# Odd row pairs copied to both partition halves, one block apart, so that one 128-row matmul does two kinds of products (dilated convolution, fp32, one core)

## The chip, the cores and the metric

The kernel runs on 1 core of one Trainium2 chip. The metric is the device time of one execution in microseconds (us), as the median of the runs shown. Times in the text that have no other source are read from one profiled execution, in us from its first instruction. Engines: PE is TensorE (PEld its weight loads), DVE VectorE, ACT ScalarE, POOL GpSimd, SP SyncE. All transfers here are issued by SP and carried by 16 DMA engines.

## The reference

```python
batch, c_in, h, w, c_out, k, dilation = 16, 64, 64, 64, 128, 3, 2
# x (16, 64, 64, 64) fp32, weight (128, 64, 3, 3) fp32, pad = 2 on each side
for b, co, ci, kh, kw:
    output[b, co] += weight[co, ci, kh, kw] * x_pad[b, ci, kh*2:kh*2+64, kw*2:kw*2+64]
# output (16, 128, 64, 64) fp32
```

16.8 MB are read (x) and 33.6 MB written; the weights have 0.3 MB.

## The kernel before

**Layout.** Two images share the 128 partitions: image m = 0 has its 64 input channels on partitions 0 to 63, image m = 1 on 64 to 127. There are 8 such pairs of images (`pb`), each cut into 4 groups of 16 rows (`g`); `G` counts the 32 groups. A pair's x is loaded as fp32 (`x32`, three buffers), cast to fp16 by ACT in chunks (`cast`, `x16`), and the output of a pair (`o`, 128 output channels on the partitions, both images side by side) is stored as fp32.

**Fewer products.** Because the dilation is 2, rows are taken two at a time: a block is two rows, and blocks alternate between even (e = 0) and odd (e = 1). With W0, W1, W2 the three kernel rows, an even output block is W0 x[odd block before] + W1 x[even] + W2 x[odd], and an odd one W0 x[even] + W1 x[odd] + W2 x[even block after]. The kernel forms s = x[even] + x[odd] on DVE (`rowsum`, `xs`) and uses five products of three taps each instead of six:

- kind 0: P = W1 s, in the PSUM tile `psP`;
- kinds 1 and 2: psA = (W2 - W1) x[odd] + W0 x[odd block before];
- kinds 3 and 4: psB = (W0 - W1) x[even] + W2 x[even block after];
- even output rows = psA + P, odd output rows = psB + P.

**Matmuls.** `product` issues, for each of the three taps j, one matmul for either half of the partitions (`hb`): 64 rows of the array by 128 columns, 512 or 496 output columns. The two halves write different PSUM banks. A kind has 6 matmuls, a group 30. Kinds 2 and 4 leave out one block of four at the upper and the lower edge of an image (`z`).

**Per group,** in program order: PE does psP, psA, psB (in group 0 psP last); ACT copies psP to SBUF (`p_sb`, since psP has one buffer) and casts up to two chunks ahead (`casts`); DVE forms the next group's row sum and then the two sums psA + p_sb and psB + p_sb into `o`. psA, psB and the weights' PSUM tiles share three buffers.

**Weights.** At the start the weights are loaded (`w32`), combined to the five kinds (`wd`, on DVE, POOL and ACT), and `turn(k)` transposes kind k with narrow matmuls (64 columns) against an identity, into both halves of the partitions; a copy by ACT or DVE puts it into `w_sb`. `dummies` are matmuls on zeros beside it.

**Order.** The schedule is written by hand (`manual_schedule`): every engine executes its instructions in program order, and SP's transfers queue in program order too. SP's list is: weights, x of pairs 0, 1, 2; x of pair 3 in group 0; from then on each pair's stores when its groups are done and further loads between them (pair 4 after group 3, pair 5 in group 7, pair 6 in group 11, pair 7 in group 15). A load into an `x32` buffer waits until the casts of the pair that had it are done. The last pair is stored in two halves; of image 1's first half the last 8 rows (`ROWS4`) go as a transfer of 124 partitions and one of 4 (`FOUR`). By the trace's landings these two run on 4 of the 16 DMA engines each, the other stores on all 16.

Of the kernel before, what the change touches and what calls it, by code (L numbers as in the profile page):

```python
# [10 lines left out]
def kernel(  # L11
# [7 lines left out]
    nc = tc.nc  # L19

    B, CI, H, W = x.shape
    CO, CI_w, KH, KW = weight.shape
# [4 lines left out]
    d = 2  # L27

    P = 128
    f32 = mybir.dt.float32  # L30
    f16 = mybir.dt.float16
# [5 lines left out]
    NG = H // GR  # L37
    NBLK = GR // 4
    NH = GR // 2 * W
    npairs = B // 2  # L40
    ngroups = npairs * NG
# [3 lines left out]
    wpool = ctx.enter_context(tc.tile_pool(name="wpool", bufs=1))  # L45
# [6 lines left out]
    apool = ctx.enter_context(tc.tile_pool(name="apool", bufs=3, space=bass.MemoryType.PSUM))  # L52
# [6 lines left out]
    x32_tiles, x16_tiles, xs_tiles, o_tiles = {}, {}, {}, {}  # L59

    def load(pb, cuts=(0, H)):
        x32_tiles[pb] = fpool.tile([P, HW], f32, tag="x32", name="x32")
        for lo, hi in zip(cuts[:-1], cuts[1:]):
            nc.sync.dma_start(  # L64
                out=x32_tiles[pb][:, lo * W : hi * W], in_=x_pair[pb, :, lo * W : hi * W]
            )

    def cast(c):
        pb, g = divmod(c, NG)
        lo, hi = chunk_rows[g]  # L70
        if g == 0:
            x16_tiles[pb] = xpool.tile([P, HW], f16, tag="x16", name="x16")
        nc.scalar.copy(  # L73
            out=x16_tiles[pb][:, lo * W : hi * W], in_=x32_tiles[pb][:, lo * W : hi * W]
        )

    def rowsum(c):
        pb, g = divmod(c, NG)
        if g == 0:
            xs_tiles[pb] = sxpool.tile([P, HW // 2], f16, tag="xs", name="xs")  # L80
        v = x16_tiles[pb][:, g * GR * W : (g + 1) * GR * W].rearrange(
            "p (b e q) -> p b e q", e=2, q=2 * W
        )
        s = xs_tiles[pb][:, g * NH : (g + 1) * NH].rearrange("p (b q) -> p b q", q=2 * W)
        nc.vector.tensor_tensor(out=s, in0=v[:, :, 0], in1=v[:, :, 1], op=add)  # L85

    w32 = wpool.tile([CO, CI * KH * KW], f32, name="w32")
    nc.sync.dma_start(out=w32, in_=weight.rearrange("o i h w -> o (i h w)"))  # L88
    load(0, (0, 2 * GR + d, H))
# [1 line left out]
    load(2)  # L91
    zero = wpool.tile([P, 512], f16, name="zero")
    nc.vector.memset(zero, 0.0)  # L93
    ident = wpool.tile([P, P], f16, name="ident")
    make_identity(nc, ident)

# [2 lines left out]
    def dummies(n):  # L99
        for _ in range(n):  # L100
            nc.tensor.matmul(out=dm[:, 0:512], lhsT=zero[:, 0:P], rhs=zero)  # L101
# [6 lines left out]
    w_sb = wpool.tile([P, NT * CO], f16, name="w_sb")  # L108
# [7 lines left out]

    wts = [apool.tile([P, 1024], f32, tag="ab", name="wt") for _ in range(3)]

    def turn(k):
        c0 = k // 3 * 512  # L120
        for j in range(KW):
            t = k * KW + j
            for r in range(2):
                nc.tensor.matmul(  # L124
                    out=wts[k % 3][r * CI : (r + 1) * CI, c0 + j * CO : c0 + (j + 1) * CO],
                    lhsT=wd[:, t * CI : (t + 1) * CI],
                    rhs=ident,
                )
        return w_sb[:, k * KW * CO : (k + 1) * KW * CO], wts[k % 3][:, c0 : c0 + KW * CO]
# [2 lines left out]
    t0 = turn(0)  # L132
    dummies(2)
    nc.vector.tensor_copy(out=t0[0], in_=t0[1])
    t1 = turn(1)
    nc.scalar.copy(out=t1[0], in_=t1[1])  # L136
    t2 = turn(2)
    nc.vector.tensor_copy(out=t2[0], in_=t2[1])
    dummies(1)
    t3 = turn(3)  # L140
    t4 = turn(4)
    dummies(1)
    nc.vector.tensor_copy(  # L143
        out=x16_tiles[0][:, 8 * W : 18 * W], in_=x32_tiles[0][:, 8 * W : 18 * W]
    )
    nc.scalar.copy(out=x16_tiles[0][:, 0 : 8 * W], in_=x32_tiles[0][:, 0 : 8 * W])  # L146
    nc.scalar.copy(out=t3[0], in_=t3[1])
    nc.vector.tensor_copy(out=t4[0], in_=t4[1])
    rowsum(0)

    ahead = [1]
# [1 line left out]
    def casts(G):  # L153
        for n in range(2 if G else 3):
            c = ahead[0]
            if c >= ngroups or c > G + (7 if c < 2 * NG else 5):
                return
            cast(c)
            ahead[0] += 1

    def product(ps, src, kind, blk0, nblk, first, last):
        for j in (1, 0, 2):
            dw = (j - 1) * d
            o0, o1 = max(0, -dw), W - max(0, dw)
            t = kind * KW + j
            for hb in range(2):
                pp = slice(hb * CI, (hb + 1) * CI)
                rhs = src(pp, dw + o0, dw + o1)
                po = ps[:, hb * NH + blk0 * 2 * W : hb * NH + (blk0 + nblk) * 2 * W]
                po = po.rearrange("p (r w) -> p r w", w=W)[:, :, o0:o1]  # L170
                nc.tensor.matmul(  # L171
                    out=po,
                    lhsT=w_sb[pp, t * CO : (t + 1) * CO],
                    rhs=rhs,
                    start=first and j == 1,
                    stop=last and j == 2,
                )

    def blocks(x16, b0, n, e):
        v = x16.rearrange("p (b e r w) -> p b e r w", e=2, r=2, w=W)  # L180
        return lambda pp, c0, c1: v[pp, b0 : b0 + n, e, :, c0:c1]
# [8 lines left out]
    def store_both(pb, r0, r1):  # L190
        nc.sync.dma_start(
            out=out_img[2 * pb : 2 * pb + 2, :, r0 * W : r1 * W].rearrange("m o q -> o m q"),
            in_=o_tiles[pb].rearrange("p (m q) -> p m q", m=2)[:, :, r0 * W : r1 * W],
        )

    FOUR = ((0, P - 4), (P - 4, P))
    ROWS4 = 8

    for G in range(ngroups):
        pb, g = divmod(G, NG)  # L200
        x16 = x16_tiles[pb]
        xs = xs_tiles[pb].rearrange("p (r w) -> p r w", w=W)
        if g == 0:
            o_tiles[pb] = opool.tile([P, 2 * HW], f32, tag="osb", name="osb")
        o = o_tiles[pb].rearrange("p (m b e q) -> p m b e q", m=2, e=2, q=2 * W)
        b0 = g * NBLK

        def summed():
            ps = ppool.tile([P, 2 * NH], f32, tag="p", name="psP")
            sv = lambda pp, c0, c1: xs[pp, g * GR // 2 : (g + 1) * GR // 2, c0:c1]  # L210
            product(ps, sv, 0, 0, NBLK, True, True)
            return ps

        if G:
            psP = summed()

        psA = apool.tile([P, 2 * NH], f32, tag="ab", name="psA")
        product(psA, blocks(x16, b0, NBLK, 1), 1, 0, NBLK, True, False)
        z = 1 if g == 0 else 0
        product(psA, blocks(x16, b0 + z - 1, NBLK - z, 1), 2, z, NBLK - z, False, True)  # L220

        psB = apool.tile([P, 2 * NH], f32, tag="ab", name="psB")
        product(psB, blocks(x16, b0, NBLK, 0), 3, 0, NBLK, True, False)
        z = 1 if g == NG - 1 else 0
        product(psB, blocks(x16, b0 + 1, NBLK - z, 0), 4, 0, NBLK - z, False, True)

        if not G:
            psP = summed()

        if not G:  # L230
            casts(0)
        p_sb = spool.tile([P, 2 * NH], f32, tag="psb", name="p_sb")
        nc.scalar.copy(out=p_sb, in_=psP)  # L233
        if G:
            casts(G)
        if G + 1 < ngroups:
            rowsum(G + 1)
        pv = p_sb.rearrange("p (m b q) -> p m b q", m=2, q=2 * W)
        for e, ps in ((0, psA), (1, psB)):
            nc.vector.tensor_tensor(  # L240
                out=o[:, :, b0 : b0 + NBLK, e],
                in0=ps.rearrange("p (m b q) -> p m b q", m=2, q=2 * W),
                in1=pv,
                op=add,
            )

        if G == 0:
            load(XF)
        if g == NG - 1 and 0 < pb < npairs - XF - 1:
            load(pb + XF + 1, (0, H) if pb < 3 else (0, H // 2, H))  # L250
        if G == NG - 2:
            store(0, 1, 0, (NG - 1) * GR)
            store(0, 0, 0, (NG - 1) * GR)
        if G == NG - 1:
            store_both(0, (NG - 1) * GR, H)
            load(XF + 1)
        elif pb == npairs - 1:
            if g % 2 == 1:
                store(pb, 0, (g - 1) * GR, (g + 1) * GR)
                if g == 1:  # L260
                    store(pb, 1, 0, 2 * GR - ROWS4)
                    store(pb, 1, 2 * GR - ROWS4, 2 * GR, FOUR)
                else:
                    store(pb, 1, (g - 1) * GR, (g + 1) * GR)
        elif g == NG - 1:
            for m in (1, 0) if pb == 1 else (0, 1):
                store(pb, m)
# [37 lines left out]
```

## Time and profile before

| what | value |
|---|---|
| device time, median of 3 runs | 128.58 us (126.77, 128.58, 128.86) |
| profiled execution, first to last instruction (span) | 126.1 us; what lies around the span is not in the profile |
| PE busy / share of the span | 104.5 us / 83%, 1000 matmuls |
| DVE, ACT, POOL busy | 90.9, 64.9, 2.2 us |
| DMA moved | 50.78 MB, 403 GB/s mean over the span |
| mean granted PE clock | 0.949 (1.00 until about 112 us, then 0.5) |
| last matmul / last DVE instruction / last DMA packet end | 108.3 / 109.6 / 124.8 us |

A row of busy tenths divides the span into 40 equal slices; 9 means 90% or more. A line of groups has the instruction's line in the kernel, engine, operation, output <- input tiles, the count, busy time, the mean of one in ns, and the engine's idle time before them. The recorded length of a matmul includes the time that it spends in the array's pipeline, so that neighbouring matmuls overlap in the records; their starts tell the rate.

### The profile page before, as it was taken

Reading aid. Unit: us, or ns where it says so; the run is one execution under the profiler, and the core shown is the slowest. Engines: PE = TensorE matmul, PEld = TensorE weight load, DVE = VectorE, ACT = ScalarE, POOL = GpSimd, SP = SyncE. Lnnn points to the kernel's source line nnn. Section 1 sums busy time; section 2 is a strip of 40 time slices with the busy share of each in tenths; the row PEclk is TensorE's granted clock in tenths of the full one; section 3 lists DMA queues with packets and bytes.
Section 4 is the critical chain, followed back from the end, with each engine's and each line's share of the span. In section 5 each row is a group of like instructions: output and inputs, shape, how many; then the busy total and the mean of one; then the engine's idle time right before and its main releaser. Section 6 shows DMA issues by size and latency. Waiting matters only on the chain.

```text
span 126.1 us, 2339 instructions
## 1 busy us (share of the span) xinstructions
PE 104.5 (83%) x1000; PEld 56.2 (45%) x1000; DVE 90.9 (72%) x103; ACT 64.9 (51%) x68; POOL 2.2 (2%) x8
## 2 busy tenths in 40 slices
PE   6965999999999999999999999999999999300000
PEld 2332555555555555555555555555555555100000
DVE  0751998988898889888988898887988887700000
ACT  4368896665666566656665666566653333000000
POOL 2400000000000000000000000000000000000000
PEclk9999999999999999999999999999999999995555
DMA  4999999999999999999999999999999999999960
GB/s 129 364 453 426 436 421 421 405 429 396 447 422 442 385 421 416 423 436 436 426 421 413 426 442 431 426 421 431 431 431 421 426 431 442 421 409 420 424 278 23
DMA packets 4594, 50.78 MB, mean 403 GB/s; under 512 B 488, under 2 KB 488, under 8 KB 1256
## 3 DMA queue, kind: packets, MB, share of 16 engines
q1 hardware_dynamic: 4584, 50.63, 95.7%
q8 instruction: 8, 0.13, 0.4%
q14 instruction: 2, 0.02, 0.0%
HBM read 17.07 MB, written 33.55 MB: 401 GB/s over the span
## 4 chain that ended last, share of the span: by engine, by line
PE 75%; DMA 6%; ACT 2%; DVE 1%; DVEq 1%; SPq 1%; issue 0%
PE psA L171 30%; PE psB L171 29%; PE psP L171 16%; DMA x<-in_x_dram 6%; ACT x L73 1%; DVE osb L240 1%; DVEq L300 1%; ACT p_sb L233 1%; SPq L64 0%; SPq L88 0%; DVEq L240 0%
## 5 line engine op out<-in xcount | busy, mean ns | idle before, releaser
L171 PEld LDWEIGHTS <-w_sb 64*128 64x128 f16 x960 | 54.2, 94 | 47.3 <-issue 1.6
L233 ACT COPY p_sb<-psP 128x1024 f32<-128x1024 f32 x32 | 32.4, 1012 | 36.9 <-issue 21.5
L240 DVE TENSOR_TENSOR osb<-psA,p_sb 128x1024 f32<-128x1024 f32 x32 | 39.2, 1225 | 13.5 <-PE psA L171 9.4
L171 PE MATMUL psA<-x,w_sb 64*128 64x496 f16 (+3 forms) x384 | 45.1, 365 | 1.0 <-ACT x L146 1.0
L171 PE MATMUL psB<-x,w_sb 64*128 64x496 f16 (+3 forms) x384 | 45.1, 365 | 0.0
L240 DVE TENSOR_TENSOR osb<-psB,p_sb 128x1024 f32<-128x1024 f32 x32 | 39.1, 1221 | 0.0
L73 ACT CAST x<-x 128x1024 f16<-128x1024 f32 (+2 forms) x31 | 32.1, 1044 | 0.5 <-DMA x<-in_x_dram 0.5
L171 PE MATMUL psP<-xs,w_sb 64*128 64x496 f16 (+1 forms) x192 | 26.0, 371 | 1.3 <-ACT p_sb L233 1.3
L85 DVE TENSOR_TENSOR xs<-x 128x512 f16<-128x512 f16 x32 | 13.3, 416 | 0.7 <-ACT x L73 0.7
L101 PE MATMUL dm<-zero 128*128 128x512 f16 x10 | 4.1, 531 | 1.2 <-DVE zero L93 1.2
L111 DVE CAST wd<-w 128x192 f16<-128x192 f32 x1 | 0.5, 497 | 2.5 <-DMA w<-in_weight_dram 2.5
L101 PEld LDWEIGHTS <-zero 128*128 128x128 f16 x10 | 1.0, 120 | 2.6 <-DVE zero L93 1.2
L124 PEld LDWEIGHTS <-wd 128*64 128x64 f16 x30 | 0.9, 109 | 1.8 <-DVE wd L111 1.2
L113 ACT ACT_TABLE_LOAD x1 | 1.3, 1283 | 0.7 <-PEq L286 0.7
L124 PE MATMUL wt<-ident,wd 128*64 128x128 f16 x30 | 1.4, 224 | 0.3 <-DVE wd L111 0.3
L113 ACT CAST wd<-w 128x192 f16<-128x192 f32 x1 | 0.5, 537 | 1.6 <-DMA w<-in_weight_dram 1.6
L146 ACT CAST x<-x 128x512 f16<-128x512 f32 x1 | 0.6, 617 | 1.1 <-DMA x<-in_x_dram 1.1
L136 ACT CAST w_sb<-wt 128x384 f16<-128x384 f32 x1 | 0.5, 479 | 1.2 <-PE wt L124 1.2
L143 DVE CAST x<-x 128x640 f16<-128x640 f32 x1 | 0.5, 494 | 0.9 <-DMA x<-in_x_dram 0.9
L93 DVE MEMSET zero<- 128x256 uint32 x1 | 0.3, 272 | 0.9 <-PEq L286 0.9
L112 POOL TENSOR_TENSOR wd<-w 128x192 f16<-128x192 f32 x1 | 0.8, 792 | 2.4 <-DMA w<-in_weight_dram 2.4
L115 POOL CAST wd<-w 128x192 f16<-128x192 f32 x1 | 0.8, 807 | 0.0
(11 smaller groups left out, 3.8 us busy)
## 6 DMA issues: line engine op xcount, KB each, us to landing
out_dram<-osb SPq DMA_DIRECT2D x12, 2048.0 KB, 18.5
x<-in_x_dram SPq DMA_DIRECT2D x6, 2048.0 KB, 16.4
out_dram<-osb SPq DMA_DIRECT2D x4, 1024.0 KB, 14.2
out_dram<-osb SPq DMA_DIRECT2D x2, 1536.0 KB, 11.7
x<-in_x_dram SPq DMA_DIRECT2D x2, 1024.0 KB, 19.4
x<-in_x_dram SPq DMA_DIRECT2D x1, 1088.0 KB, 5.8
x<-in_x_dram SPq DMA_DIRECT2D x1, 960.0 KB, 7.6
out_dram<-osb SPq DMA_DIRECT2D x1, 768.0 KB, 16.6
```

Source lines behind the costliest of these rows:

```text
L73: nc.scalar.copy(out=x16_tiles[pb][:, lo * W : hi * W], in_=x32_tiles[pb][:, lo * W : hi * W])
L85: nc.vector.tensor_tensor(out=s, in0=v[:, :, 0], in1=v[:, :, 1], op=add)
L101: nc.tensor.matmul(out=dm[:, 0:512], lhsT=zero[:, 0:P], rhs=zero)
L112: nc.gpsimd.tensor_tensor(out=wdv[:, 3], in0=wv[:, 0], in1=wv[:, 1], op=sub)
L113: nc.scalar.copy(out=wdv[:, 2], in_=wv[:, 0])
L115: nc.gpsimd.tensor_copy(out=wdv[:, 4], in_=wv[:, 2])
L124: nc.tensor.matmul(out=wts[k % 3][r * CI : (r + 1) * CI, c0 + j * CO : c0 + (j + 1) * CO], lhsT=wd[:, t * CI : (t + 1) * CI], rhs=ident,)
L146: nc.scalar.copy(out=x16_tiles[0][:, 0 : 8 * W], in_=x32_tiles[0][:, 0 : 8 * W])
L171: nc.tensor.matmul(out=po, lhsT=w_sb[pp, t * CO : (t + 1) * CO], rhs=rhs, start=first and j == 1, stop=last and j == 2,)
L233: nc.scalar.copy(out=p_sb, in_=psP)
L240: nc.vector.tensor_tensor(out=o[:, :, b0 : b0 + NBLK, e], in0=ps.rearrange("p (m b q) -> p m b q", m=2, q=2 * W), in1=pv, op=add,)
L300: with _tile.TileContext(nc) as tc:
```

## The change

- `shift(c, engines)` copies the odd blocks of chunk c into a new fp16 ring `xo` of four slots (one for each group of a pair): for either image m once to its own half of the partitions, in place, and once to the other half, one block later. That is four copies of 64 partitions x 512 elements for each group (384 where the first block stays zero), given to GpSimd, GpSimd, ScalarE and GpSimd in this order, two groups ahead; for chunk 0 to DVE, GpSimd, ScalarE and DVE. Two memsets on GpSimd clear the first block of slot 0.
- `stacked(ps, g)` takes the place of the two `product` calls of psA: one matmul over all 128 rows for each tap and image, whose weights have kind 1 in the image's own half and kind 2 in the other. psA has 6 matmuls instead of 12, and always four blocks.
- `turn(1)` and `turn(2)` build the mixed weights (`HALVES`); they come after turns 3 and 4 now, and group 0 does psB before psA.
- Casts run at most 4 chunks ahead of the group (7 in the first two pairs and 5 later before).
- `ROWS4` is 6 instead of 8: the transfers on 4 DMA engines have 6 rows, and the one before them 26 instead of 24.

```diff
+    xo_ring = wpool.tile([P, NG * 2 * NH], f16, name="xo")
+    xo = xo_ring.rearrange("p (g m n) -> p g m n", g=NG, m=2)
+
+    def shift(c, engines):
+        pb, g = divmod(c, NG)
+        v = x16_tiles[pb].rearrange("p (b e q) -> p b e q", e=2, q=2 * W)
+        it = iter(engines)
+        for m in range(2):
+            own = slice(m * CI, (m + 1) * CI)
+            for late in range(2):
+                lanes = own if not late else slice((1 - m) * CI, (2 - m) * CI)
+                z = 1 if late and g == 0 else 0
+                to = xo[lanes, g, m, z * 2 * W :].rearrange("p (b q) -> p b q", q=2 * W)
+                at = g * NBLK - late + z
+                src = v[own, at : at + NBLK - z, 1]
+                eng = next(it)
+                if eng is nc.scalar:
+                    eng.copy(out=to, in_=src)
+                else:
+                    eng.tensor_copy(out=to, in_=src)
...
+    nc.gpsimd.memset(xo[CI:P, 0, 0, 0 : 2 * W], 0.0)
+    nc.gpsimd.memset(xo[0:CI, 0, 1, 0 : 2 * W], 0.0)
...
+    HALVES = ((0, 0), (1, 2), (2, 1), (3, 3), (4, 4))
+
     def turn(k):
         c0 = k // 3 * 512
         for j in range(KW):
-            t = k * KW + j
             for r in range(2):
+                t = HALVES[k][r] * KW + j
...
     nc.vector.tensor_copy(out=t0[0], in_=t0[1])
+    t3 = turn(3)
+    nc.scalar.copy(out=t3[0], in_=t3[1])
+    t4 = turn(4)
+    nc.vector.tensor_copy(out=t4[0], in_=t4[1])
+    dummies(1)
     t1 = turn(1)
-    nc.scalar.copy(out=t1[0], in_=t1[1])
     t2 = turn(2)
-    nc.vector.tensor_copy(out=t2[0], in_=t2[1])
-    dummies(1)
-    t3 = turn(3)
-    t4 = turn(4)
     dummies(1)
...
-    nc.scalar.copy(out=t3[0], in_=t3[1])
-    nc.vector.tensor_copy(out=t4[0], in_=t4[1])
+    nc.scalar.copy(out=t1[0], in_=t1[1])
+    nc.vector.tensor_copy(out=t2[0], in_=t2[1])
+    shift(0, (nc.vector, nc.gpsimd, nc.scalar, nc.vector))
     rowsum(0)
...
-            if c >= ngroups or c > G + (7 if c < 2 * NG else 5):
+            if c >= ngroups or c > G + 4:
...
+    def stacked(ps, g):
+        for j in (1, 0, 2):
+            dw = (j - 1) * d
+            o0, o1 = max(0, -dw), W - max(0, dw)
+            for m in range(2):
+                t = (1 + m) * KW + j
+                rows = lambda v: v.rearrange("p (r w) -> p r w", w=W)
+                nc.tensor.matmul(
+                    out=rows(ps[:, m * NH : (m + 1) * NH])[:, :, o0:o1],
+                    lhsT=w_sb[:, t * CO : (t + 1) * CO],
+                    rhs=rows(xo[:, g, m])[:, :, dw + o0 : dw + o1],
+                    start=j == 1,
+                    stop=j == 2,
+                )
...
-    ROWS4 = 8
+    ROWS4 = 6
...
-        psA = apool.tile([P, 2 * NH], f32, tag="ab", name="psA")
-        product(psA, blocks(x16, b0, NBLK, 1), 1, 0, NBLK, True, False)
-        z = 1 if g == 0 else 0
-        product(psA, blocks(x16, b0 + z - 1, NBLK - z, 1), 2, z, NBLK - z, False, True)
+        def even():
+            ps = apool.tile([P, 2 * NH], f32, tag="ab", name="psA")
+            stacked(ps, g)
+            return ps
+
+        if G:
+            psA = even()
...
+        if not G:
+            psA = even()
...
         if G:
             casts(G)
+        for c in range(G + 1 if not G else G + 2, min(G + 3, ngroups)):
+            shift(c, (nc.gpsimd, nc.gpsimd, nc.scalar, nc.gpsimd))
         if G + 1 < ngroups:
             rowsum(G + 1)
```

## The prediction

> **What bounds the kernel now.** I read the page first, then busy times by stretch, then the transfers, then the startup.
>
> ```profile
> span 126.1 us, 2339 instructions
> ...
> PE 104.5 (83%) x1000; PEld 56.2 (45%) x1000; DVE 90.9 (72%) x103; ACT 64.9 (51%) x68; POOL 2.2 (2%) x8
> ...
> DMA  4999999999999999999999999999999999999960
> ...
> q1 hardware_dynamic: 4584, 50.63, 95.7%
> ```
>
> The DMA row is at 9 from the second slice to the last but two: the 16 DMA engines never run dry. The stretches of the end (PE, PEld, DVE, ACT, POOL busy, then granted clock, DMA share, GB/s) show what is left when the computing is over:
>
> ```profile
> 96.00:108.00 12.00, 12.00 (x120) 6.51 (x116) 10.26 (x12) 4.05 (x4) 0.00 (x0) 1.00 1.01 431
> 108.00:112.00 4.00, 0.28 (x4) 0.00 (x0) 1.63 (x2) 0.00 (x0) 0.00 (x0) 1.00 0.99 420
> 112.00:116.00 4.00, 0.00 (x0) 0.00 (x0) 0.00 (x0) 0.00 (x0) 0.00 (x0) 0.64 0.98 411
> 116.00:120.00 4.00, 0.00 (x0) 0.00 (x0) 0.00 (x0) 0.00 (x0) 0.00 (x0) 0.50 1.02 427
> 120.00:124.00 4.00, 0.00 (x0) 0.00 (x0) 0.00 (x0) 0.00 (x0) 0.00 (x0) 0.50 0.51 213
> ```
>
> PE is full until 108.3 and stops; the DMA engines go on for 16 us. So PE sets when the stores are issued, and the queue sets the end. How deep the queue is, is read from issue to landing (2 MB alone need 4.9 us: 8 packets of 16 KB on each engine, 611 ns each):
>
> ```profile
> out_dram<-osb SPq DMA_DIRECT2D x12, 2048.0 KB, 18.5
> ```
>
> The packet records (start, length, size) give the rest: on one engine a packet starts 3 to 4 ns before its predecessor's recorded end, so from 14 us on they can be strung into 16 chains. Their ends: eight engines that fetched 16 KB of PE's instructions once each 121.6 to 123.8; the four with the 2 KB packets of the split store 122.6 to 123.5; three others 120.0 to 120.5; one 124.84. That last one fetched nothing and has no 2 KB packets: its 16 KB packets have a median of 634 ns, all others' 611. It sets the end, and 1.3 us of closing work follow.
>
> **PE's streaming: nothing gained.** The chain in order of time, one group of 16 rows:
>
> ```profile
> 25.34 1.27 PE psA L171 x12
> 26.61 1.27 PE psB L171 x12
> 27.88 0.63 PE psP L171 x6
> ```
>
> The 12 matmuls of psA are six pairs on 64 rows each; the two of a pair start 19 ns apart and pairs follow at 210 to 216 ns, so the array is full already. Six 128-row matmuls at that spacing take the same 1.27 us. Lost: at the first group of a pair of images kind 2 used to stream three blocks (psA 1.11 us), now four, +0.16. Gained: 12 of 60 PE instructions per group, 384 of 2007, so 6 fetches of 256 instead of 8. A fetch costs its engine its own 0.93 us and 0.40 on the packet behind it, 1.33 us; two fewer spread over 16 engines are worth 2 x 1.33 / 16 = 0.17 us on a random engine, nothing on one that had none.
>
> **Switching between 64-row and 128-row matmuls,** twice per group, is new in the steady stage. The startup has changes of array shape (wt is 64 columns wide, dm full):
>
> ```profile
> 5.03 0.53 PE L124 MATMUL wt<-ident,wd 128*64 128x128 f16 x12
> ...
> 5.49 0.39 PE L101 MATMUL dm<-zero 128*128 128x512 f16 x1
> ...
> 5.81 0.53 PE L124 MATMUL wt<-ident,wd 128*64 128x128 f16 x12
> ```
>
> By single records the last wt starts at 5.338 and dm at 5.489: 151 ns where wt pairs follow at 55, 96 lost. From dm to the next wt are 320 ns where 512 columns take 216: 104 lost, with the weights ready (POOL done at 5.24). I take 0.10 us a switch, 0.20 a group. Bounds: 0, if splitting by rows drains less than splitting by columns, and 0.21, a whole matmul exposed. A gain is excluded, since pairs already run at streaming rate. The Trainium skill, TensorEngine Tiling (Array Packing), "Tiling Modes", says that changing the tiling mode drains the engine; it gives no price, so the sum can't be made by it; the 96 and 104 ns here agree with a drain.
>
> **POOL's three copies per group** (64x512 f16) have no row. One element costs 100 ns (const memset), 128 cost 294 (affine select, f16 to f16), so 1.52 ns each: 0.87 us for 512, 2.6 a group, under PE's 3.37. Lower bound from the plain memset (205 ns for 128): 0.52. Upper from the 192-element cast (807): 3.7 ns each, 1.98. But these rows overlap DVE's:
>
> ```profile
> 3.70 0.79 POOL L112 TENSOR_TENSOR wd<-w 128x192 f16<-128x192 f32 x1 [2.40 <-DMA w<-in_weight_dram]
> 4.07 0.79 DVE L114 TENSOR_TENSOR wd<-w 128x192 f16<-128x192 f32 x1
> ...
> 4.44 0.81 POOL L115 CAST wd<-w 128x192 f16<-128x192 f32 x1
> ```
>
> L112 ends at 4.50, L114 at 4.86, L115 at 5.24: 0.36 and 0.38 apart. They take turns, so the cast alone is 0.38, (0.38 - 0.10) / 192 = 1.5 ns an element again. I keep 0.87.
>
> **ACT's copy** (64x512): 0.62, L146's 617 ns for 512 elements. ACT per group 1.01 + 1.05 + 0.62 = 2.7, under 3.37. **DVE** per group 0.42 + 2 x 1.22 = 2.86; if the row sum waits for a POOL copy under way, half of 0.87 in three quarters of cases adds 0.33: 3.2, still under.
>
> **Start.** Turns 3 and 4 go ahead of 1 and 2: the same copies and matmuls in another order. Turn 4 waits for POOL's wd of 5.24; all are through by about 6.9, before x lands at 7.0. POOL's two memsets (128 elements, 0.2 us each) lie in its idle time from 1.3 to 3.7. psB goes first; the copies for psA (DVE twice at most 0.42, POOL 0.87, ACT 0.62) run under its 1.27. ACT's 0.62 and the three casts push p_sb(0) from 11.1 to 11.5; behind it wait psP(1) (one buffer) and DVE: group 1 starts 0.4 late. Two more ACT copies (1.2) and casts for which the load is there delay p_sb(2), so the first stores, issued at 19.97, come at about 21. The load ahead of them lands first at 23.1 and a transfer starts 1.0 us after its issue (0.74 to 1.75 at the start): hidden.
>
> **Casts at most 4 ahead** free x32 later: load 5 is issued in group 7 instead of 6, near 35.6 instead of 30.47. The load before it lands first at 37.78: 1.2 us left. Loads 6 and 7 have over 3.
>
> **Sum.** Stores of the seventh pair (97.29): 0.4 start + 27 groups x 0.20 + 6 x 0.16 = 6.8 later, 104.1, first packets 105.1. The transfer ahead lands on the engines between 101.45 and 106.23. The first to be free idles 4 us; it ended 4.8 before the last and can afford that. The slow one is free at about 105.9 and never waits. Last stores (109.66): 0.4 + 31 x 0.20 + 7 x 0.16 = 7.7 later, 117.4; the slow engine has work until 120.4. So PE's loss is hidden by 0.8 us; without that cover each microsecond costs one. Rows: 26 rows instead of 24 on all engines are 4 KB more each, 8 x (6656 - 6144) bytes at 26.7 per ns: +0.15; the lowest four lose 32 x 20 ns: -0.47 net. The last engine is none of these four: +0.15. Fetches -0.17. Net 0.0: span 126.1. The three runs are 126.77, 128.58, 128.86; the span is 0.7 under the lowest, and the median lies 1.8 above that one, which I read as a later slow engine. It hides PE's loss better still. **128.6.**
>
> **Rivals.** Two per cent either way (126.0, 131.1) is about what a measurement of this kernel can tell from no change.
>
> *The lighter DMA load shows* (0.13): where the last engine is one that had a fetch or the split store, it loses 1.33 or 0.47: 127.3. For: 12 of 16 engines are such. Against: not the one that ended last here.
>
> *Switches cost 0.21* (0.09): 27 x 0.42 + 1.4 = 12.7, stores at 110.0. From their first packet to the end lie 124.84 - 105.9 = 18.9: 111.0 + 18.9 + 0.15 = 130.1 against 124.84, +5.2: 133.8. It costs from 0.115 a switch (the 0.8 us over 54 switches) and passes 2% at 0.16. Against: 0.10 measured twice.
>
> *POOL and DVE taking turns makes DVE the bound* (0.07): if every row sum waits for a whole copy, DVE needs 2.86 + 0.87 = 3.73 a group, against 3.09 now on average: 28 x 0.64 + 0.4 = 18.3, stores at 115.6, end 135.6: +10.8, 139.4. It costs from 3.35 a group and passes 2% at 3.44. For: L114. Against: POOL is idle a quarter of the time. The Trainium skill, SBUF — State Buffer, "Who interferes with whom", has it as an exclusive lock between a DVE instruction with two SBUF inputs and a GpSimd one that reads SBUF; the 0.36 and 0.38 agree.
>
> *The copies don't run ahead* (0.03): at 1.98 each POOL needs 5.9 a group, past 200 us; or each copy waits for the matmuls on the other slots of xo, so that 2.6 of copying and 1.3 of psA alternate, 3.9 a group, near 150. Against: the turns above; and a cast at 7.91 (ACT, 1.05) writes rows of x16 while psA's matmuls read others from 7.68.
>
> **Numbers.** Forecast 0.68, spread 126.4 to 130. Range 126.4 to 132: beyond it lie most of the last three and 0.04 below. Faster: 0.06 (a third of the first rival, a little of run spread). Slower: 0.19 (the last three). Same: 0.75.
>
> **What would show it.** Right: L171 x576 with 64 rows and x192 of 128 in a new line; gaps near 0.1 us at each change; PE ending near 116 and DMA still at 9 to about 120; six fetches; xs (416 ns) longer by 0.2 to 0.4 beside copies of 0.8 to 1.0. Wrong: a 7 or less in the DMA row before 110, PE waiting for xo, DVE without idle time, or a POOL copy over 1.1 us.

## Result and profile after

The changed kernel takes 131.75 us (median of 6 runs, 130.06 to 132.08) against 127.63 (6 runs, 126.44 to 128.86): ratio 1.0349, 95% interval 1.0289 to 1.0409. It is slower. Forecast were 128.6 us and no change; 131.75 lies at the far end of the stated range (126.4 to 132), on the side to which the prediction gave a chance of 0.19. In later comparisons the kernel before had medians of 126.95, 126.83 and 126.62, and the changed kernel 130.65.

The ratios and their intervals leave disturbed runs out, so a ratio can differ a little from that of the medians. In the runs listed with their span, the time is about 1.8 us above it. The profiled execution of the changed kernel is 131.49 us at a span of 129.7. By the same difference the profile of before, span 126.1, stands for about 127.9, not for the 128.58 that the prediction set it equal to.

From the page of the changed kernel: the span, the busy tenths of the DMA engines in 40 slices of 3.24 us, the queue of the instruction fetches, and the issues of 2 MB stores:

```profile
span 129.7 us, 2149 instructions
...
DMA  4999999999999899999999999999999849999991
...
q8 instruction: 6, 0.10, 0.3%
...
out_dram<-osb SPq DMA_DIRECT2D x12, 2048.0 KB, 13.4
```

The row that was 9 from the second slice to the last but two now has an 8 and a 4 near 105 us: there the DMA engines ran out of work (the text calls this the hole). A 2 MB store lands 13.4 us after its issue, where it took 18.5: the queue is 5 us shallower. The fetches of instructions are six, as forecast. The end of the changed kernel by stretches (us; PE, PEld, DVE, ACT, POOL busy; granted clock, DMA share, GB/s):

```profile
100.00:104.00 4.00, 4.00 (x36) 1.64 (x32) 3.51 (x4) 3.27 (x5) 2.17 (x4) 1.00 0.87 373
104.00:107.00 3.00, 3.00 (x24) 1.14 (x22) 2.66 (x4) 1.80 (x3) 1.48 (x3) 1.00 0.52 218
107.00:116.00 9.00, 9.00 (x66) 3.41 (x62) 7.22 (x8) 3.65 (x4) 0.00 (x0) 1.00 0.96 410
116.00:120.00 4.00, 1.49 (x14) 0.50 (x12) 2.38 (x2) 0.00 (x0) 0.00 (x0) 1.00 1.02 427
120.00:124.00 4.00, 0.00 (x0) 0.00 (x0) 0.00 (x0) 0.00 (x0) 0.00 (x0) 0.75 1.02 312
124.00:129.00 5.00, 0.00 (x0) 0.00 (x0) 0.00 (x0) 0.00 (x0) 0.00 (x0) 0.50 0.59 247
```

Two losses stand in the last two columns. At 104 to 107 us the engines are half idle (0.52). The stores of the seventh pair are issued at 105.40 and their first packets start at 106.24; the transfer ahead lands on the engines between 103.46 and 105.76, so they wait. At 120 to 124 us they are busy all the time (1.02) and yet move 312 GB/s instead of 427: packets are slow there. The prediction had no such thing.

The steady stage is as forecast. The chain in order of time (start, us), one group of 16 rows:

```profile
30.62 0.63 PE psP L199 x6
31.25 1.38 PE psA L214 x6
32.63 1.37 PE psB L199 x12
```

psA and psB took 1.27 each, so each switch costs about 0.105. By single records the starts of the last matmul ahead of a switch and the first behind it are 305 ns apart on both sides of psA, where 207 to 210 is the pace. The copies and the row sum, 20 to 100 us; the last line is the row sum of the kernel before, over its whole span:

```profile
L108 POOL COPY xo<-x 64x512 f16<-64x512 f16 x62 | 37.8, 610 | 34.7 <-ACT x L73 32.1 <-POOL xo L108 0.3
L106 ACT COPY xo<-x 64x512 f16<-64x512 f16 x24 | 14.8, 615 | 0.6
L85 DVE TENSOR_TENSOR xs<-x 128x512 f16<-128x512 f16 x24 | 12.7, 527 | 0.0
...
L85 DVE TENSOR_TENSOR xs<-x 128x512 f16<-128x512 f16 x32 | 13.3, 416 | 0.7 <-ACT x L73 0.7
```

POOL waits 32 of the 80 us for casts, and in the list of waits PE waits for none of them: the copies hold nothing up here.

### The profile page after: what moved, and what is told of

It is laid out like the page before. It is cut to its first block, busy times and chain, and to the rows that moved or that the text cites. A ratio compares the mean times of both kernels' runs of the same rounds, so it can differ in the third digit from the quotient of the medians.

```text
span 129.7 us, 2149 instructions
## 1 busy us (share of the span) xinstructions
PE 114.6 (88%) x808; PEld 44.3 (34%) x808; DVE 95.5 (74%) x105; ACT 87.3 (67%) x100; POOL 58.8 (45%) x104
## 4 chain that ended last, share of the span: by engine, by line
PE 85%; DVE 3%; DMA 2%; ACT 1%; issue 0%; DVEq 0%
PE psA L214 34%; PE psB L199 32%; PE psP L199 16%; DMA w<-in_weight_dram 2%; DVE osb L290 2%; PE wt L151 2%; PE dm L126 1%; ACT p_sb L281 1%; DVE w_sb L165 0%; DVE wd L136 0%; DVEq L290 0%
## 5 line engine op out<-in xcount | busy, mean ns | idle before, releaser
L108 POOL COPY xo<-x 64x512 f16<-64x512 f16 (+1 forms) x94 | 56.2, 598 | 43.9 <-ACT x L73 37.3
L214 PE MATMUL psA<-xo,w_sb 128*128 128x496 f16 (+1 forms) x192 | 46.2, 376 | 0.0
L199 PEld LDWEIGHTS <-w_sb 64*128 64x128 f16 x576 | 25.4, 94 | 39.4 <-issue 15.0
L214 PEld LDWEIGHTS <-w_sb 128*128 128x128 f16 x192 | 16.2, 98 | 27.8 <-issue 12.7
L106 ACT COPY xo<-x 64x512 f16<-64x512 f16 x32 | 19.6, 615 | 0.8
L85 DVE TENSOR_TENSOR xs<-x 128x512 f16<-128x512 f16 x32 | 16.6, 519 | 0.3 <-ACT x L73 0.3
L126 PE MATMUL dm<-zero 128*128 128x512 f16 x10 | 5.0, 624 | 1.2 <-DVE zero L116 1.2
L151 PE MATMUL wt<-ident,wd 128*64 128x128 f16 x30 | 2.2, 312 | 0.6 <-DVE wd L136 0.5
L151 PEld LDWEIGHTS <-wd 128*64 128x64 f16 x30 | 1.6, 161 | 2.8 <-DVE wd L136 1.4
L165 DVE CAST w_sb<-wt 128x384 f16<-128x384 f32 x1 | 0.6, 558 | 1.2 <-PE wt L151 1.2
## 6 DMA issues: line engine op xcount, KB each, us to landing
out_dram<-osb SPq DMA_DIRECT2D x12, 2048.0 KB, 13.4
```

Of the source, the lines that this page charges most:

```text
L106: eng.copy(out=to, in_=src)
L108: eng.tensor_copy(out=to, in_=src)
L151: nc.tensor.matmul(out=wts[k % 3][r * CI : (r + 1) * CI, c0 + j * CO : c0 + (j + 1) * CO], lhsT=wd[:, t * CI : (t + 1) * CI], rhs=ident,)
L199: nc.tensor.matmul(out=po, lhsT=w_sb[pp, t * CO : (t + 1) * CO], rhs=rhs, start=first and j == 1, stop=last and j == 2,)
L214: nc.tensor.matmul(out=rows(ps[:, m * NH : (m + 1) * NH])[:, :, o0:o1], lhsT=w_sb[:, t * CO : (t + 1) * CO], rhs=rows(xo[:, g, m])[:, :, d ...
```

## Experiments: is it the copies, the switches, or the time of the seventh stores?

The theory: PE needs more time per group, the stores of the seventh pair come after the queue has run dry, and from there the end is tied to their issue. The rival: the copies on POOL and ACT and their contention with DVE slow the kernel.

**Copies kept, stacking undone.**

```diff
-            t = kind * KW + j
             for hb in range(2):
+                t = (3 - kind if hb and kind in (1, 2) else kind) * KW + j
...
-            stacked(ps, g)
+            z = 1 if g == 0 else 0
+            product(ps, blocks(x16, b0, NBLK, 1), 1, 0, NBLK, True, False)
+            product(ps, blocks(x16, b0 + z - 1, NBLK - z, 1), 2, z, NBLK - z, False, True)
```

> The changed kernel with psA computed as before, by pairs of 64-row matmuls from x16; the four copies per group into xo are still made, and so are the new start order, the cast limit and the 6 rows. Queue theory (PE's pace of 3.385 us a group, of which 0.21 are the two switches, lets the DMA queue run dry before the stores of the seventh pair): groups back at 3.17 us, seventh pair's stores issued at 97.3 + 1.5 of late start = 98.8 instead of 105.4, DMA busy throughout, time within 1% of before (127.6, so 126.5 to 129). Copy theory (the copies' load on POOL, ACT and SBUF costs the time): no change from the changed kernel, 131 to 132. Stall theory (slow DMA packets, 2.5 us more per engine, come with the change whatever PE does): about 130.

Measured: 127.52 us, ratio 1.0035 (0.9994 to 1.0075). Copies, memsets, the new order of turns, the 4-ahead casts and 6 rows are all in, and the time is back. The row sum even took 605 ns in the mean, and it didn't matter: DVE has idle time. The DMA row has no hole; the stores of the seventh pair went out at 97.56.

```profile
DMA  4999999999999999999999999999999999999971
...
L85 DVE TENSOR_TENSOR xs<-x 128x512 f16<-128x512 f16 x32 | 19.4, 605 | 0.5 <-ACT x L73 0.5
```

**No copies, no stacking, but more PE work:** the kernel before with one or two extra pairs of 64-row matmuls per group (0.216 us a pair).

```diff
+            for _ in range(1):   # 2 in the second kernel
+                for hb in range(2):
...
+                    nc.tensor.matmul(out=ps[:, hb * NH : (hb + 1) * NH], lhsT=w_sb[pp, KW * CO - 2 * CO : KW * CO - CO],
+                        rhs=xs[pp, g * GR // 2 : (g + 1) * GR // 2, :].rearrange("p r w -> p (r w)"), start=True, stop=True)
             product(ps, sv, 0, 0, NBLK, True, True)
```

> The kernel before with one more pair of 64-row matmuls (512 columns) per group, written to psP and overwritten by the product that follows: PE gets 0.216 us longer per group, with no switch, no copy and no change to the start. Queue theory: stores of the seventh pair issued at 97.3 + 27 x 0.216 = 103.1, first packets 104.1; on the four engines with the split store 21.5 us of packets are left from there (16 x 0.607 + 8 x 0.306 + 8 x 0.231 + 32 x 0.081 + 16 x 0.306), end 125.6 and span 126.9 against 126.1: +0.8 us, hardly to be told from before (127 to 129.5). Copy theory and stall theory: as before, 127.6.

> The kernel before with two more pairs of 64-row matmuls per group (0.432 us). Queue theory: the cover is used up, stores of the seventh pair at 97.3 + 27 x 0.432 = 109.0, first packets 110.0, end 131.5, span 132.8: +6.7 us, time 133 to 135; the first extra pair costs 1 us or less, the second 5 to 6. Copy theory and stall theory: as before, 127.6, since nothing is copied and PE is not what ends.

Measured: one pair 130.70 us, ratio 1.0289 (1.0214 to 1.0364); two pairs 135.79, ratio 1.0727 (1.0654 to 1.0800). Both are above what was expected (127 to 129.5, and 133 to 135): the loss of the first pair was taken as nearly covered, and its profile began late (first stores at 21.36). A bare 0.216 us per group does most of what the change did, and the queue runs dry at the same place (stores issued at 104.08, transfer ahead landed 102.61 to 105.52; slices of 3.22 us):

```profile
DMA  4999999999999999999999999999999879999981
```

With two pairs it also runs dry one store earlier (the 4 in the middle of the row; slices of 3.35 us):

```profile
DMA  5999999999999999999999999997499519999991
```

From the issue of the seventh stores to the last packet are 23.2 us in the changed kernel, 23.6 and 23.7 in these two: where the queue is dry the end moves one for one with that issue. In the kernel before, where the queue is never dry, it is 27.5.

**The small parts alone:** the kernel before with casts at most 4 ahead and 6 rows on the lowest engines.

```diff
-            if c >= ngroups or c > G + (7 if c < 2 * NG else 5):
+            if c >= ngroups or c > G + 4:
...
-    ROWS4 = 8
+    ROWS4 = 6
```

> The kernel before with two small parts of the change alone: casts at most 4 ahead, and 6 rows instead of 8 on the four engines. Queue theory: loads 5 to 7 are issued later, but the queue still covers them and PE's pace stays, so the time is that of before within 0.5% (126.5 to 127.5). If the later loads cost the time (slow packets near 32 and 42 us are larger in the changed kernel), 128 to 129.

Measured: 126.99 us, ratio 1.0017 (0.9978 to 1.0056). Nothing, as forecast.

**One switch per group:** the stacked matmuls of two neighbouring groups put side by side.

```diff
-        if G:
+        even_first = G % 2 == 1
+        if G == 1:
             psP = summed()
...
-        if G:
+        if G and even_first:
             psA = even()
+            if G > 1:
+                psP = summed()
...
             psA = even()
-        if not G:
             psP = summed()
+        elif not even_first:
+            psP = summed()
+            psA = even()
...
-        for e, ps in ((0, psA), (1, psB)):
+        for e, ps in ((0, psA), (1, psB)) if even_first else ((1, psB), (0, psA)):
```

> The changed kernel with the order of products alternating: even groups psB, psP, psA, odd groups psA, psP, psB, so that the psA of two neighbouring groups lie side by side and PE changes between 64 and 128 rows once per group instead of twice (groups 0 and 1 as before). So far the runs in which the queue ran dry ended 23.2 to 23.7 us after the issue of the seventh pair's stores. Queue theory: pace 3.385 - 0.105 = 3.28 us a group, 27 x 0.105 = 2.8 earlier, but psP comes later within a group, which costs the last group of the pair about 0.8: stores at 103.4, time 2.0 less than the changed kernel, 129.5 to 130. If the 128-row matmuls themselves were slow, and not the changes, the pace and the time would stay (131.7).

Measured: 129.64 us, ratio 1.0194 (1.0111 to 1.0278). By the chain four groups take 12.95 us (19.65 to 32.60) where the changed kernel needs 13.37: 0.42 for four switches taken away, 0.105 each. From the issue of the first stores to that of the seventh pair's, 25 groups, it is 77.32 us in the kernel before, 83.35 in the changed one and 81.08 here: 2.27 / 25 = 0.09 a group (this includes what the new order inside a group does to the stores). The profiled execution began late (first stores at 23.12) and is the slowest of the four, 130.33.

## Experiments: why the end is later than its stores

With the dry queue alone, 105.40 instead of 97.29 doesn't give the end: from the first packets behind the hole (about 106.4) an engine has 16 packets of 607 ns, 8 of 306 and 16 more of 306, and 8 of 250: 19.06 us, the prediction's 18.9. The four engines of the split store (the two transfers of `FOUR`, 186 KB and 6 KB) have 32 packets of 62 ns on top, 2.0 us. In the kernel before the ends of the engines are 4.8 us apart and those four are not the last; a hole sets all sixteen level, and then they are: twelve engines of the changed kernel end at 126.60 to 126.89, four at 127.97 to 128.54.

**The changed kernel without the split store.**

```diff
-                    store(pb, 1, 0, 2 * GR - ROWS4)
-                    store(pb, 1, 2 * GR - ROWS4, 2 * GR, FOUR)
+                    store(pb, 1, 0, 2 * GR)
```

> The changed kernel with the last pair's half image stored in one transfer over all 16 engines (no 26 + 6 rows). Queue theory with the split store as a term of its own: once the queue has run dry, all engines start level, and the four with 32 packets of 1536 bytes need 2.0 us more than the others; without the split all need 16 x 0.607 + 16 x 0.306 + 16 x 0.306 = 19.5 instead of 21.05 on those four: 1.5 us less, 130.0 to 130.4. If the slow packets seen 15 us after those stores (1.1 us) come from the split, another 1 us less, 129. If the end is set by something else (copies, start), no change: 131.7.

Measured: 129.39 us, ratio 1.0145 (1.0053 to 1.0236). The hole is there (the DMA row of its page), the slow packets are not (its stretch of 120 to 124 us):

```profile
DMA  4999999999999999999999999999999938999994
```

```profile
120.00:124.00 4.00, 0.00 (x0) 0.00 (x0) 0.00 (x0) 0.00 (x0) 0.00 (x0) 0.65 1.01 426
```

The engines end together: 15 of them between 124.33 and 124.63, the last at 124.85, 20.9 us after the issue at 103.92, where the changed kernel has 23.15. So the split and the slow packets cost 2.2 us from the issue on. The profiled execution is the fastest of the four (127.92) and began early (first stores at 20.55), so of the 2.4 us between the medians a part can be the start's.

**The same step on the kernels without stacking.** The edit is the same; the first is the kernel before, the second the one with an extra pair.

> The kernel before, with the two last rows of the second half stored by one transfer instead of a large one over 16 engines and a small one over 4. Where the queue is never dry the engines finish ragged, and the split only moves work among them. Theory (the split costs 2 us only when all engines run level after a dry queue): within 1% of the kernel before, 126 to 128 us, and few slow packets after 110 us as in the kernel before. Rival (the split costs its 2 us on four engines in any case): 125 to 126 us, faster by 1% or more.

> The kernel before with one extra pair of 64-row products in each group (0.216 us of TensorE, no copies, no stacking; the output stays right) and with the last stores unsplit. The same kernel with the split store took 130.7 us. The queue runs dry before the stores of the 7th pair, issued near 104 us in a profile. Theory (the slow packets near 120 us come only where the split store meets engines that a dry queue has set level, and the split itself is 2 us on four engines): no slow packets after 110 us, last packet 20.5 us after the issue, about 124.6, and 127.5 to 128.5 us. Rival (the slow packets follow the dry queue in any case, some 15 us later): a cluster of slow packets near 120 us again, last packet 21.5 to 22 us after the issue, 128.8 to 129.5 us.

Measured: the kernel before without the split 127.43 us, ratio 1.0055 (1.0027 to 1.0084): covered, the split store earns half a per cent. With the extra pair 128.57, ratio 1.0138 (1.0095 to 1.0181), where the same kernel with the split had 1.0289: in a dry queue it costs 1.5%. Again no slow packets behind the hole (its DMA row, and two of its stretches):

```profile
DMA  5999999999999999999999999999999959999990
```

```profile
116.00:120.00 4.00, 0.00 (x0) 0.00 (x0) 0.24 (x1) 0.00 (x0) 0.00 (x0) 1.00 1.01 426
120.00:124.00 4.00, 0.00 (x0) 0.00 (x0) 0.00 (x0) 0.00 (x0) 0.00 (x0) 0.53 0.88 371
```

The 371 come at a share of 0.88, engines that had ended: 422 at full share, no slow packets. Thirteen engines end between 123.45 and 123.60, 20.4 to 20.6 us after the issue at 103.04, as the theory has it; the last ends at 125.43, 22.4 us after it, which is later than the theory has it. What held it is not shown (a fetch of PE's instructions, 0.94 us at 108.82, lies behind the hole in this profile).

Over all profiles of this study: packets over 1.15 times the median of their size, after 115 us, number 57 to 71 in all seven kernels with a hole and the split store, and 0 in the seven others (split without a hole, hole without the split, neither). That the two together bring these is shown. They lie where the small packets of the split store run: in the changed kernel at 120.3 to 122.8 us, its 1.5 KB packets at 120.5 to 123.6, and 39 of the 50 packets of 8 KB that start between 120.5 and 122.8 are slow too. In the kernel before the small packets run at 115.1 to 118.5, and none is slow. Why packets slow down there is not shown. Nor are a hole and a split store the only way to slow packets: all fourteen profiles have a spell near 42 us, where neither is at work, of 0.36 us on the mean engine in the kernel before and 1.34 in the changed one.

## Experiments: the start

The first stores went out at 22.05 where 21 was forecast. The transposes of the weights (TensorE, 4 to 8.6 us) in the kernel before, the changed one, and the changed one without the split, whose start is the same code:

```profile
L124 PE MATMUL wt<-ident,wd 128*64 128x128 f16 x30 | 1.4, 224 | 0.3 <-DVE wd L111 0.3
```

```profile
L151 PE MATMUL wt<-ident,wd 128*64 128x128 f16 x30 | 2.2, 312 | 0.6 <-DVE wd L136 0.5
```

```profile
L151 PE MATMUL wt<-ident,wd 128*64 128x128 f16 x30 | 1.6, 240 | 0.5 <-DVE w_sb L165 0.3 <-DVE wd L136 0.2
```

The same matmuls take 224, 312 and 240 ns: TensorE begins at half its later rate and keeps it until about 4 us, 9 us and 5 us. The profile's row of the granted clock shows 9 in these slices. First stores: 19.97, 22.05 and 20.55 us. The Trainium skill, TensorE: Matmul & The Clock Gate, Part 1, "What's actually happening", has a clock gate that opens after a busy window of 3.4 us which runs free, so that the moment varies from run to run by 500 ns either way; the half rate agrees, but in nine of the fourteen profiles here it ends at 4 to 6 us and in five at 8 to 11 us, a far wider spread.

**Other PSUM tiles for the weights:** in the changed kernel turn 1 waited for DVE's copy of turn 4 out of the same tile (6.77 to 7.33 us).

```diff
+    SLOT = (0, 3, 4, 1, 2)
...
-        c0 = k // 3 * 512
+        c0 = SLOT[k] // 3 * 512
+        wt = wts[SLOT[k] % 3]
```

> The changed kernel with one PSUM tile of the weights' transposes exchanged, so that turn 1 no longer waits for the copy of turn 4 (which shares its tile). Queue theory: the first product starts about 1 us earlier, everything behind it on PE too, stores of the seventh pair at 104.4 instead of 105.4, and the time falls by the same 1 us, to 130.7. Copy theory and stall theory: the start is hidden behind the loads, no change (131.7).

Measured: 129.96 us (129.90 to 130.44), ratio 1.0246 (1.0201 to 1.0291). The first stores left at 20.45, the seventh pair's at 103.82. The half rate ended by 5.5 us in its profile, so the gain can't be given to the edit: the run above had 20.55 without it.

**The changed kernel again, and with more dummies ahead of the weights.**

```diff
-    dummies(6)
+    dummies(8)
```

> The changed kernel once more, for its start. In the profiles so far the TensorE matmuls of the start run at half their later rate until 4.4 to 5 us or until 8 to 10 us, and the first stores go out at 20.5 us or at 22 to 23 us. Theory (this draw decides the start): the time falls into two groups, near 130.0 us where the half rate ends by 5 us and near 131.7 us where it lasts to 8 us or more; the profiled run shows the first stores at 20.5 in the first case and at 22 in the second. Rival (the start of the changed kernel is always late, by its order of turns): all runs near 131.7 us, first stores at 22 us whatever the rate.

> The changed kernel with eight instead of six dummy matmuls ahead of the transposes of the weights: TensorE has no pause of 0.4 to 0.8 us at 3.9 us, where it waits for the weights. Theory (the pause decides whether the half rate ends near 4.5 us or is drawn out to 8 us or more): half rate over by 5 us in the profile, first stores issued at 20.4 to 20.8 us, all runs at 129.7 to 130.4 us. Rival (the rate has nothing to do with the pause): the same two groups of times as the changed kernel, or up to 0.4 us more where the extra matmuls delay the transposes.

Measured: again, 132.14, 130.28, 130.67 and 130.63 us, ratio 1.0323 (1.0267 to 1.0379). The profiled one is that of 132.14: half rate until about 10.4 us, first stores at 22.57. That fits two groups, and one profile alone stands behind it. With eight dummies 130.43 us (130.01 to 131.57), ratio 1.0293 (1.0250 to 1.0335); half rate until 5.6 us, first stores at 21.12. It is inside neither expectation cleanly: no run is near 132, one is at 131.57, and the pause of TensorE doesn't decide alone (0.29 us went with 10 us of half rate in the one-switch kernel, 0.39 with 5 us in the kernel that follows). What draws the length of the half rate stays open.

**All three together:** other tiles, one switch, no split.

> The changed kernel with all three: the earlier start, one change of rows per group, and no split store. Queue theory: seventh pair's stores at 105.4 - 1.6 - 2.0 = 101.8, and 21.6 us from there give 123.4, below the 124.6 at which the DMA engines end when they never run dry: the time is that of before within 1% (126 to 128). Copy theory: still 130 or more.

Measured: 128.37 us, ratio 1.0103 (1.0032 to 1.0173). The stores go out at 102.30, and the last packet ends at 124.73, where that of before ended at 124.84. The row shows no hole, but the stretch of 100 to 104 us still has a small one (0.94), and nine engines end level, at 122.72 to 122.86, as behind a hole:

```profile
DMA  4999999999999999999999999999999999999990
```

```profile
100.00:104.00 4.00, 4.00 (x29) 1.76 (x26) 3.67 (x4) 3.09 (x4) 1.99 (x3) 1.00 0.94 397
```

Two thirds of the loss are back, and it still is about 1% slower: the profile of before stands for 127.9 us, 1 us above its median there, and this one for 127.94, near the lower of its four runs. None of these kernels beats the one before.

## Why the prediction was wrong, by its steps

What held:
- **Switches** of 0.10 twice a group, read from the startup: 0.105 by the chain, and 0.105 by that of the one-switch kernel. The startup's changes are between 64 and 128 columns, these between 64 and 128 rows; that both cost the same was not known.
- **The group** and the lost short product: four groups take 12.36 us before (two of 3.17, two of 3.01) and 13.37 after (three of 3.38, one of 3.23). That is 4 x 0.21 + 0.16. For the 25 groups between the first and the seventh stores it makes 25 x 0.21 + 6 x 0.16 = 6.2 us; by the issues it is 6.03.
- **ACT's copy** 0.615 us (0.62), **load 5** issued at 36.68 (35.6) and hidden, **six fetches**, and **rows** at no price.
- **Loose, without effect:** POOL's copy 0.61 us (0.87), the row sum 0.10 longer (0.33). The row sum is longer beside POOL's copies, as a lock between DVE and POOL would have it, and DVE had room.

What failed, in the order of size:

1. **The remainder behind the hole.** "From their first packet to the end lie 124.84 - 105.9 = 18.9" was the slow engine's, which had no split packets. On the engines that have them it is 21.05, and 1.1 more passed in slow packets (4 us at 312 instead of 427 GB/s are 1.08 lost): 22.15 from 106.4 to 128.55. The term was too small by 3.2 us. The kernel with one extra pair shows this step apart from the start: its stores were issued at 104.08, the 104.1 of the forecast, and its slow engine, free at 105.02, went straight on to the new packets, as the prediction had it. The last packet ended at 127.70 all the same: four engines end at 126.83 to 127.70 and the other twelve by 125.87.
2. **The cover.** "The slow one is free at about 105.9 and never waits", so that 0.8 us were left over, looked at that engine and at the first one to be free, not at the four with the split store. The slow engine is in the changed kernel's profile too (from 75.6 us on, a string of 16 KB packets, nearly all of 625 to 667 ns, that join end to start), but it is free at 104.98 there and the stores' packets come at 106.24, so even it waits. With the split store deciding, stores must be out near 101.7 for the end of 124.84 (124.84 - 23.15); forecast were 104.1. The cover was some 2.4 us short, not 0.8 long.
3. **The start.** "Group 1 starts 0.4 late", first stores near 21: 22.05, seventh stores at 105.40 instead of 104.1. Where the half rate ends early the sum was right (103.92 and 103.82 in two kernels), and the time is then near 130.0.
4. **The level.** The 1.8 us between 126.77 and 128.58 were read as a later slow engine that would hide still more. They are spread between runs: all runs of the kernel before, 49 of them, lie between 126.38 and 128.86. What spreads them is not shown.

Together they are the difference of the two ends: stores issued 8.11 us later (105.40 against 97.29: 6.03 from the groups, 2.08 from the start), and 23.15 from there to the end instead of 27.55, which is 8.11 - 4.40 = 3.71 us. The sign named as proof of error, a 7 or less in the DMA row before 110 us, is the 4 at 105. Of the rivals, none was it: switches cost 0.10, DVE kept its idle time, the copies ran ahead, and the lighter load on the DMA engines showed nowhere. The mechanism of the rival with the dear switches, though, a queue that runs dry and then costs one for one, is what happened, at the switch price of the forecast.

## What to carry to other kernels

A queue that is never dry hides slower computing only up to a limit, and the engine that ends last today doesn't give it. For every engine take the later of two moments, when it is free and when the delayed work reaches it, and add what it then still has to move; the greatest of these sums is the end. The prediction followed the engine that ended last and the first to be free, and not the four with small packets. Once the queue has a hole, its engines start level, and every piece that sits on a few of them (here a store split off for four) comes straight on top of the end: the split earned 0.5% in the covered queue and cost 1.5% in the dry one.

## What was not expected of the hardware

- Changing between 64-row and 128-row matmuls costs about 105 ns each time in the steady stage too (305 ns from start to start where 207 to 210 is the pace).
- With a hole in the queue and four engines on 1.5 KB packets, packets slow down for some 3 us, while the small packets run: 1.05 us lost on the mean engine in the changed kernel (312 GB/s from 120 to 124 us, against 426 without the split).
- One of the 16 DMA engines is slower: in all fourteen profiles one string of 16 KB packets between 76 and 92 us takes 639 to 652 ns a packet (medians), where the others take 611.
- TensorE's half rate at the start lasts to 5 or to 10 us with the same code, and the changed kernel's first stores move by 2 us with it (20.55 and 22.57).
